# RMSNorm with a sigmoid gate on one core: two row groups of 48 and 16 become 44 and 20

## The chip, the core and the metric

The kernel runs on one NeuronCore of a Trainium2 chip. The metric is device time in microseconds (us), the median of several runs of the whole program. The profile gives one execution: its span runs from the first to the last profiled instruction, and the time of that same execution is a little longer.

Of the engines, four matter here. ACT (ScalarE) and DVE (VectorE) do the arithmetic, POOL (GpSimd) does two small operations for each unit of rows, and SP (SyncE) does no arithmetic: it issues DMA transfers and waits on semaphores. The transfers themselves are run by 16 DMA engines. The tensor engine is not used.

## The reference

```python
def reference(x, gamma, eps):              # x: 16 x 1024 x 512 float32, gamma: 512 ones, eps 1e-5
    rms = np.sqrt(np.mean(x ** 2, axis=-1, keepdims=True) + eps)
    x_norm = x / rms * gamma
    return (x_norm * (1.0 / (1.0 + np.exp(-x_norm)))).astype(np.float32)
```

There are 16384 rows of 512 float32, 2 KB each: 33.55 MB are read and 33.55 MB are written.

## The kernel before

**Tiling.** Each of the 128 partitions holds 128 rows of 2 KB. These rows are cut into *groups* (line 28): 32, 48, 16 and 32 rows. A group of n rows is one block of DRAM, and partition p owns the n rows that follow each other there from p times n on (`dram`, line 100). So n also sets how far apart in DRAM the data of neighbouring partitions lie, the *pitch*: 32 rows are 64 KB, 48 rows 96 KB, 16 rows 32 KB. In SBUF the rows lie in a ring of 96 row slots, `xb` (lines 29 and 108): row 96 takes the slot of row 0. All is done in place.

**Transfers.** `loads` and `stores` (lines 30 to 32) list pieces as (first row, rows); a piece may not cross the edge of a group (the assertion in `dram`). Every piece is one DMA over all 128 partitions; n rows of a partition are contiguous in DRAM and in SBUF. In the text, load 64 is the piece that begins at row 64, store 0 the store that begins at row 0, and so on.

**SP's order** (`order`, lines 33 to 37) is written out by hand. SP issues loads 0, 4 and 8, gamma, then loads 16 to 75. Then it waits until load 64 has landed (line 166), issues store 0 (line 121) and, right behind it, load 80. It waits until store 0 is done, since loads 96 to 125 go into the slots of rows 0 to 31 (line 169), and issues these three. It waits until load 112 has landed and issues the other five stores. Store t waits, besides, until all units that it touches are finished (`ends`, line 56, on the semaphore `s_swish`). At the end SP waits for all stores (line 170).

**Units.** The arithmetic goes by units of 8 rows, 16 units in all. For a unit, ACT squares and sums 6 of its rows (line 215) and DVE the other 2 (line 251; the first unit is split 4 and 4); POOL adds eps and raises to the power -0.5 (lines 183 and 189); DVE multiplies each row by its factor and by gamma (line 260); ACT runs Silu over the whole unit (lines 225 and 245). ACT squares unit k+2 ahead of the Silu of unit k. PE's queue does nothing but wait, for each unit k, for the loads that begin within it, and pass that on to ACT as `s_land`.

The change touches the lists in lines 28 to 37; everything else is worked out from them.

Of the kernel before, what the change touches and what calls it, by code (L numbers as in the profile page):

```python
# [9 lines left out]
def kernel(  # L10
# [14 lines left out]
    of = out.flatten_outer_dims()  # L25
    R, D = xf.shape

    groups = [32, 48, 16, 32]
    ring = 96
    loads = [(0, 4), (4, 4), (8, 8), (16, 8), (24, 8), (32, 16), (48, 16), (64, 11), (75, 5)]  # L30
    loads += [(80, 16), (96, 16), (112, 13), (125, 3)]
    stores = [(0, 32), (32, 32), (64, 16), (80, 16), (96, 24), (120, 8)]
    order = [("load", a) for a in (0, 4, 8)] + [("gamma", 0)]
    order += [("load", a) for a in (16, 24, 32, 48, 64, 75)]
    order += [("landed", 64), ("store", 0), ("load", 80)]
    order += [("stored", 0), ("load", 96), ("load", 112), ("load", 125)]
    order += [("landed", 112)] + [("store", a) for a in (32, 64, 80, 96, 120)]
    early = 2
    cn = 8
    own = 2  # L40
# [285 lines left out]
```

## Time and profile before

| what | us |
|---|---|
| median of 3 runs | 159.67 (159.59 to 159.82) |
| the profiled execution, its own time | 159.75 |
| its span, first to last instruction | 158.4 |
| busy in the span: DVE, ACT, POOL | 107.7, 115.7, 42.9 |

The trace also holds each DMA packet: start, duration and bytes. In this kernel a packet is the rows of one piece for one partition, so a piece has 128 packets, 8 on each of the 16 DMA engines. The next table is put together from these records, by size and order of time; times are from the span's start.

| piece | rows | first packet starts, us | last packet ends, us | packet: median ns | mean ns |
|---|---|---|---|---|---|
| load 0 | 4 | 1.02 | 4.38 | 309 | 367.6 |
| load 4 | 4 | 4.11 | 7.03 | 309 | 310.7 |
| load 24 | 8 | 16.23 | 21.62 | 611 | 611.2 |
| load 32 | 16 | 21.09 | 31.33 | 1215 | 1215.9 |
| load 48 | 16 | 30.77 | 41.04 | 1217 | 1216.7 |
| load 64 | 11 | 40.48 | 47.74 | 840 | 840.6 |
| load 75 | 5 | 47.18 | 50.84 | 389 | 388.7 |
| store 0 | 32 | 50.27 | 70.31 | 2418 | 2448.9 |
| load 80 | 16 | 69.82 | 80.46 | 1213 | 1225.2 |
| load 96 | 16 | 79.53 | 90.14 | 1213 | 1214.4 |
| load 112 | 13 | 89.21 | 98.02 | 987 | 988.8 |
| load 125 | 3 | 97.10 | 99.87 | 234 | 235.1 |
| store 32 | 32 | 99.32 | 119.19 | 2422 | 2430.3 |
| store 64 | 16 | 118.74 | 128.87 | 1218 | 1217.5 |
| store 80 | 16 | 128.45 | 138.55 | 1220 | 1220.9 |
| store 96 | 24 | 138.20 | 153.05 | 1820 | 1820.8 |
| store 120 | 8 | 152.74 | 157.91 | 611 | 613.2 |

The 16 engines don't run in step. The column of first starts follows the engine that is furthest ahead, that of last ends the one that is furthest behind; the first is below the line above's last end because the engines are apart by 0.3 to 0.9 us. All packets together took 2510.5 us, 156.9 us for each of the 16 engines.

### The profile page before, as it was taken

To read this page: it belongs to the slowest core of one execution; us is meant where nothing else is said; L and a number is where in the kernel's file an instruction comes from. 1 tells how busy PE (TensorE), PEld (TensorE's weight loads), DVE (VectorE), ACT (ScalarE), POOL (GpSimd) and SP (SyncE) were. 2 spreads that over 40 slices of the span, in tenths; PEclk is the share of its full clock that TensorE was granted. 3 is DMA by queue.
4 is the path that set the end of the run, shared out by engine and by line. 5 is a ranking of instruction groups with operands and counts; after the bars stand their busy time and mean duration, and the time that the engine had idled before them with its cause. 6 is when DMAs were issued, how large, how long until landed. Compare 5 with 4: busy or idle time off the path is not lost. (4 is left out here: it accounts for less than half of the span.)

```text
span 158.4 us, 844 instructions
## 1 busy us (share of the span) xinstructions
DVE 107.7 (68%) x198; ACT 115.7 (73%) x205; POOL 42.9 (27%) x38
## 2 busy tenths in 40 slices
DVE  0051899798989889898925989989898995000000
ACT  3608389999999999999459999999999385400000
POOL 1031426060524426060601433516061500000000
DMA  7999999999999979799999999996969999999997
GB/s 257 451 416 443 422 488 439 397 406 497 389 395 565 463 331 530 314 381 480 406 406 472 399 430 400 550 513 281 530 298 488 406 397 455 538 397 397 397 397 331
DMA packets 2744, 67.12 MB, mean 424 GB/s; under 512 B 308, under 2 KB 308, under 8 KB 440
## 3 DMA queue, kind: packets, MB, share of 16 engines
q1 hardware_dynamic: 2744, 67.12, 99.1%
HBM read 33.56 MB, written 33.55 MB: 424 GB/s over the span
## 5 line engine op out<-in xcount | busy, mean ns | idle before, releaser
L260 DVE SCALAR_TENSOR_TENSOR xb<-xb,rstd,gamma_sb 128x512 f32 (+1 forms) x128 | 86.1, 745 | 0.0
L215 ACT ACTIVATE junk<-xb 128x512 f32 (+1 forms) x94 | 54.6, 581 | 13.1 <-ACTq L98 11.3
L225 ACT ACTIVATE xb<-xb x14 | 50.5, 3604 | 0.7 <-ACTq L98 0.7
L251 DVE SCALAR_TENSOR_TENSOR junk_v<-xb 128x512 f32 (+1 forms) x34 | 22.1, 689 | 23.0 <-DVEq L98 23.0
L189 POOL TENSOR_TENSOR rstd<-aeps,neg_half 128x8 f32<-128x8 f32 x16 | 31.7, 1984 | 1.3
L183 POOL TENSOR_SCALAR aeps<-ms 128x8 f32<-128x8 f32 x16 | 10.4, 648 | 79.1 <-DVE junk_v L251 79.1
L215 ACT ACTIVATION_READ_ACCUMULATOR junk<-xb 128x1 f32 x94 | 17.7, 188 | 0.0
L245 ACT ACTIVATE xb<-xb 128x4096 f32<-128x4096 f32 x2 | 7.2, 3616 | 5.0 <-DVE xb L260 5.0
L251 DVE DVE_READ_ACCUMULATOR junk_v<-xb 128x1 f32 x34 | 2.8, 82 | 0.0
L227 ACT ACT_TABLE_LOAD x1 | 1.3, 1283 | 1.9 <-PEq L62 1.9
L269 DVE LOAD_MASK_SELECT gamma_sb<-gamma x1 | 0.0, 14 | 2.0 <-DMA gamma<-in_gamma_dram 2.0
L178 POOL MEMSET gamma<- 128x512 f32 x1 | 0.5, 524 | 1.5 <-POOLq L62 1.5
L269 DVE STREAM_SHUFFLE gamma_sb<-gamma 128x512 f32<-128x512 f32 x1 | 0.7, 719 | 0.0
L307 POOL MEMSET const-float32-0.0<- 128x1 f32 x1 | 0.1, 98 | 0.2 <-issue 0.2
L179 POOL MEMSET neg_half<- 128x8 f32 x1 | 0.1, 104 | 0.0
L307 POOL MEMSET const-bfloat16-1.0<- 128x1 bf16 x1 | 0.1, 103 | 0.0
L307 POOL MEMSET const-uint8-127<- 128x1 uint8 x1 | 0.1, 102 | 0.0
L307 POOL MEMSET const-float32-1.0<- 128x1 f32 x1 | 0.1, 99 | 0.0
## 6 DMA issues: line engine op xcount, KB each, us to landing
xb<-in_x_dram SPq DMA_DIRECT2D x4, 4096.0 KB, 29.9
out_dram<-xb SPq DMA_DIRECT2D x2, 4096.0 KB, 29.8
xb<-in_x_dram SPq DMA_DIRECT2D x3, 2048.0 KB, 14.1
out_dram<-xb SPq DMA_DIRECT2D x1, 6144.0 KB, 22.4
xb<-in_x_dram SPq DMA_DIRECT2D x1, 3328.0 KB, 27.0
xb<-in_x_dram SPq DMA_DIRECT2D x1, 2816.0 KB, 43.1
xb<-in_x_dram SPq DMA_DIRECT2D x2, 1024.0 KB, 6.0
out_dram<-xb SPq DMA_DIRECT2D x1, 2048.0 KB, 21.9
```

The source lines that it names most:

```text
L178: nc.gpsimd.memset(gamma4, 0.0).then_inc(s_zero, 1)
L179: nc.gpsimd.memset(neg_half, -0.5).then_inc(s_half, 1)
L183: nc.gpsimd.tensor_scalar(out=aeps[k % 2], in0=ms[min(k, 1)], scalar1=eps_f, scalar2=None, op0=ALU.add,),
L189: nc.gpsimd.tensor_tensor(out=rstd[:, k * cn : (k + 1) * cn], in0=aeps[k % 2], in1=neg_half, op=ALU.pow),
L215: nc.scalar.activation(out=dummies[j], in_=rows[j], func=AF.Square, scale=inv_d**0.5, accum_out=sums[:, j : j + 1],)
L225: nc.scalar.activation(out=rows, in_=rows, func=AF.Silu).then_inc(s_swish, 1)
L227: nc.scalar.preload_act_table_set("silu_and_others")
L245: nc.scalar.activation(out=rows, in_=rows, func=AF.Silu), s_norm, n + 1
L251: ins = nc.vector.scalar_tensor_tensor(out=junk_v[j], in0=rows[j], scalar=inv_d, in1=rows[j], op0=ALU.mult, op1=ALU.mult, accum_out=to[:, ...
L260: ins = nc.vector.scalar_tensor_tensor(out=rows[j], in0=rows[j], scalar=factors[j], in1=gamma_sb, op0=ALU.mult, op1=ALU.mult,)
L269: need(nc.vector.stream_shuffle(gamma_sb, gamma4, [0] * 32), s_gld, 16).then_inc(s_gamma, 1)
L307: nc = _bacc.Bacc("TRN2", target_bir_lowering=False, num_devices=1)
```

## The change

Rows 32 to 79 and 80 to 95, the second and third group, become rows 32 to 75 and 76 to 95. The pitch of the second group goes from 96 KB to 88 KB, that of the third from 32 KB to 40 KB. Load 64 has 12 rows instead of 11, and the load behind it has 4 rows from row 76 on instead of 5 from row 75 on; it is now the beginning of the third group. Load 80 is as long as before, but covers rows 4 to 19 of a group of 20 instead of a whole group. The stores of rows 64 to 95 are 12 and 20 rows instead of 16 and 16. The numbers of loads, stores and waits and their order are the same.

```diff
-    groups = [32, 48, 16, 32]
+    groups = [32, 44, 20, 32]
     ring = 96
-    loads = [(0, 4), (4, 4), (8, 8), (16, 8), (24, 8), (32, 16), (48, 16), (64, 11), (75, 5)]
+    loads = [(0, 4), (4, 4), (8, 8), (16, 8), (24, 8), (32, 16), (48, 16), (64, 12), (76, 4)]
     loads += [(80, 16), (96, 16), (112, 13), (125, 3)]
-    stores = [(0, 32), (32, 32), (64, 16), (80, 16), (96, 24), (120, 8)]
+    stores = [(0, 32), (32, 32), (64, 12), (76, 20), (96, 24), (120, 8)]
     order = [("load", a) for a in (0, 4, 8)] + [("gamma", 0)]
-    order += [("load", a) for a in (16, 24, 32, 48, 64, 75)]
+    order += [("load", a) for a in (16, 24, 32, 48, 64, 76)]
     order += [("landed", 64), ("store", 0), ("load", 80)]
     order += [("stored", 0), ("load", 96), ("load", 112), ("load", 125)]
-    order += [("landed", 112)] + [("store", a) for a in (32, 64, 80, 96, 120)]
+    order += [("landed", 112)] + [("store", a) for a in (32, 64, 76, 96, 120)]
```

## The prediction

> **What bounds the kernel now.** I read first the page's busy times, slices and DMA queue, then SyncE's waits, then the windows around the two places where loads give way to stores.
>
> ```profile
> DVE 107.7 (68%) x198; ACT 115.7 (73%) x205; POOL 42.9 (27%) x38
> DMA  7999999999999979799999999996969999999997
> q1 hardware_dynamic: 2744, 67.12, 99.1%
> ```
>
> No compute engine is busy for more than 73% of the span, while the packets of the one DMA queue took 99.1% of what 16 DMA engines have. A slice (3.96 us) counts a packet where it starts, so the dips of the DMA row at 55 to 67 and 107 to 119 us, among the longest packets (2.4 us), need not be idle time. To tell these apart I counted, from the packet records, how many packets were in flight at each moment. From 2 us to 99 us and from 99.6 us to 157.6 us the mean is 16.0, with no loss. The engines have nothing to do for the first 1.02 us; at 99.0 to 99.6 us they lose 0.12 us of 16 engines' time; and the last packet ends at 157.92. So the span is 1.02 (first issue to first packet) + 156.9 (packets, mean of the engines) + 0.46 (last packet to SyncE's last wait), which is 158.38; the execution's own 159.75 has 1.37 more around the span, and stands 0.08 above the median of 159.67. To change the time one has to change the sum of the packets, or starve the engine that is furthest behind.
>
> ```profile
> SPq L166 <- DMA xb<-in_x_dram: 68.3, 2, 42.1
> SPq L121 <- ACT xb L245: 25.9, 2, 20.9
> SPq L115 <- DMA out_dram<-xb: 21.8, 1, 21.8
> SPq L121 <- ACT xb L225: 10.5, 1, 10.5
> ```
>
> SyncE's own waits: L166 is the wait for a landed load, 42.1 us for load 64 and 26.1 for load 112. These and the wait for store 0 (L115, 21.8) hold SyncE back, but the queue behind it is full meanwhile. The stores' waits for ACT (L121) are for the last three stores, issued at 109.8, 131.1 and 136.4 us; the packet table has their first packets at 128.45, 138.20 and 152.74, so the closest of them is 7.1 us early. ACT's work is hidden there.
>
> ```profile
> 48.37 0.35 SPq L121 DMA_DIRECT2D out_dram<-xb  x1
> 98.48 38.26 SPq L121 DMA_DIRECT2D out_dram<-xb  x5
> xb<-in_x_dram SPq DMA_DIRECT2D x1, 2816.0 KB, 43.1
> xb<-in_x_dram SPq DMA_DIRECT2D x1, 1280.0 KB, 45.7
> ```
>
> The first two lines are from the timeline of SyncE: store 0 is issued at 48.37, store 32 at 98.48. The other two, from the issues, are load 64 (2816 KB), which lands 43.1 us after its issue at 5.13, so at 48.2, and load 75 (1280 KB).
>
> **The change part by part.** *Sizes.* A packet's duration goes linearly with its rows: 8 rows 611 ns, 13 rows 987, so 75.2 ns a row. Load 64 with 12 rows: 987 - 75.2 = 911.8 ns; 8 packets on each engine are 7.29 us, against 8 x 840.6 = 6.72: it ends 0.57 later. The load behind it, 4 rows: load 4's 310.7 x 8 = 2.49 us, against 8 x 388.7 = 3.11. Together 9.78 against 9.83: -0.05 us. Stores: from 8 rows (613.2) to 16 (1217.5) a row is 75.5 ns, so 12 rows are 915 and 20 rows 1519; 8 x 2434 = 19.48 us, against 8 x (1217.5 + 1220.9) = 19.51: -0.03 us. The number of packets stays, and so do their bytes. Sum of the sizes: -0.08 us.
>
> *The first switch to stores.* Its wait changes hands. ACT's Silu of unit 3 runs 44.75 to 48.35 and the landing was at 48.27, so store 0 waited for both alike; now the landing comes at 48.27 + 0.57 = 48.84 and decides. SyncE begins store 0 some 0.1 us later, at 48.94 (before 48.37), and load 80, queued behind it, moves as well from 48.77 to 49.34. How soon could store 0 begin? Where the queue had run dry, at the second switch, its first packet came 99.32 - 98.48 = 0.84 us after the issue: so from 49.78 on. The engine furthest ahead began load 75 at 47.18; now it begins the 4 rows at 47.75 and is through with them at 50.24. A margin of 0.46 us is left of the 1.06 (50.27 against 48.37 + 0.84), and the engine furthest behind has 0.6 more. Price on the path: 0. If the cover is gone: each further us of delay in the landing costs about 0.5 us. Load 80 has the 19 us of store 0 as its cover, then.
>
> *Compute.* Units 8 and 9 wait for loads 64 and 76, both landed by about 51.4; ACT squares unit 8 from 62.62 and unit 9 from 69.80, 11 us later. Unit 10 waits for load 80, whose end doesn't move. Price 0.
>
> *The stores of rows 64 to 95.* Both pieces need the same units as before (through unit 9, and through unit 11), so SyncE issues them at the same times, right behind store 32 and at 109.83. The second comes up 4 x 75.5 x 8 = 2.4 us earlier, at 126.0 instead of 128.45, still 16 us after its issue. The stores behind it keep their places. Price 0.
>
> *The pitch.* No row has 88 or 40 KB. The nearest rows are the same 16-row packets at 96 KB (load 48, 1216.7), at 64 KB (load 96, 1214.4) and at 32 KB (load 80, median 1213, mean 1225.2): the medians are within 0.3%, and the mean of load 80 is raised by its first packets, right behind the last writes of store 0. Store rows say the same: 1217.5 at 96 KB, 1220.9 at 32 KB. The bound against the change is load 80 over load 96, 0.9%, or store 0's mean over its median, 1.3%; the bound for it is that these excesses vanish: (2448.9 - 2418) x 8 = 0.25 us at store 0, 0.10 at load 80, 0.10 at store 32, 0.45 in all. I take 0, since medians at three pitches agree.
>
> [...]
>
> Sum: the execution's own 159.75 - 0.08 = 159.67; less the 0.08 by which it stood above the median, 159.6 us.
>
> **The rivals.** *A, the pitch costs (slower).* At the new pitch the 16 streams of a piece fall into each other's way in DRAM. The place is every packet of rows 32 to 95: 39.1 us of loads (8 x the means of loads 32 to 80) and 39.0 of stores, 78.1 in all. At 0.9% it is 0.7 us, 160.3; at 1.3%, 1.0 us, 160.6. It decides from 0.32 / 78.1 = 0.4%, 5 ns in a 16-row packet. For it: nothing hides it, since no engine is ever idle. Against it: rates at 32, 64 and 96 KB agree. *B, the cover is too short (slower).* If landing and issue take over 1 us longer than here, all engines starve before store 0; 1 us longer idles them by some 0.5 us: 160.2. Against it: at the second switch the cover is shorter still (3 rows, 1.88 us), and the loss there, 0.12 us, falls on the engines ahead, while the one furthest behind went on to 99.87 with no gap. *C, the turn is smoother (faster).* The 0.25 and 0.10 us lost at store 0's end and load 80's start (67 to 71 us) go, because load 80 begins elsewhere in DRAM: 159.3. For it: the excess is real, on nearly all engines. Against it: the turn from writes to reads stays in the program.
>
> **How the numbers follow.** Within 0.2% is 0.32 us, about what a measurement of this kernel can tell, as the three runs are 0.23 apart. The forecast, no change, gets 0.45. A gets 0.29 and B 0.08, together slower 0.37. C gets 0.18. The likeliest case's own range is 159.4 to 159.9. The range goes down to 159.2 (all 0.45 us won back) and up to 160.7 (A at 1.3%), and leaves out some 0.15, most of it above.
>
> **What would show it.** Right: SyncE's store 0 begins at about 48.9, its first packets still at about 50.2; packets of load 64 near 912 ns, of store 76 near 1519; packets in flight stay at 16 through 47 to 71 us; the last packet ends near 157.9. Rival A would show 16-row packets of loads 32 and 48 above 1222 ns; B a hole before store 0's first packets; C a mean of store 0 near 2418. I am wrong if the median leaves 159.35 to 160.0, above all with packets unchanged in length.

## The result, and the profile after

The changed kernel takes 160.26 us (median; 160.09 to 160.41 over 7 executions), the kernel before 159.73 over its 7. The ratio is 1.0033, 95% interval 1.0023 to 1.0043: slower by 0.53 us, where no change was forecast. The profiled execution took 160.11 us, with a span of 158.7; it is 0.36 us longer than that of the kernel before (159.75), and its last packet ends 0.45 us later.

Three parts of the page of the changed kernel: busy times, the DMA row in 40 slices, the DMA queue.

```profile
DVE 107.7 (68%) x198; ACT 115.7 (73%) x205; POOL 42.8 (27%) x38
...
DMA  7999999999999969959999899999969979999997
...
q1 hardware_dynamic: 2744, 67.12, 99.0%
```

Nothing here tells the two kernels apart: the same work, the same 2744 packets, a queue that is as full. The loss has to be looked for in time. SyncE's timeline and two of its waits, changed kernel:

```profile
48.64 0.35 SPq L121 DMA_DIRECT2D out_dram<-xb  x1
49.03 23.23 SPq L115 DMA_DIRECT2D xb<-in_x_dram  x4
98.94 38.24 SPq L121 DMA_DIRECT2D out_dram<-xb  x5
```

```profile
SPq L166 <- DMA xb<-in_x_dram: 69.2, 2, 42.6
...
SPq L115 <- DMA out_dram<-xb: 21.5, 1, 21.5
```

Store 0 is issued 0.27 us later than before (48.64 against 48.37), since the landing of the longer load 64 now comes last. By the second switch, SyncE is 0.46 us late (98.94 against 98.48). In between lies the arrival of load 80, for which ACT waits ahead of unit 10. First ACT's timeline in the kernel before, then in the changed one (start, duration, instruction, idle time ahead of it):

```profile
80.96 0.60 ACT L215 ACTIVATE junk<-xb 128x512 f32 x1 [3.88 <-ACTq L98]
```

```profile
81.41 0.60 ACT L215 ACTIVATE junk<-xb 128x512 f32 x1 [4.65 <-ACTq L98]
```

Load 80 is 0.45 us late there. The DMA queue in the stretch in which store 0 gives way to load 80 (window from 67 to 73 us; length, busy times with instructions, tensor clock, DMA share and GB/s, counted by the packets that start in it), before and after:

```profile
67.00:73.00 6.00, 6.00 (x12) 6.00 (x12) 2.68 (x2) 1.00 1.05 431
```

```profile
67.00:73.00 6.00, 5.84 (x10) 6.00 (x12) 2.68 (x2) 1.00 1.07 415
```

The engines are as busy, and they move less: packets are longer. By the packets in flight, an engine stands idle for only 0.04 us in the mean from 66 to 73 us. The packet records say which packets are longer. As in the table of the kernel before:

| piece | last packet ends, us: before, after | packet mean ns: before, after |
|---|---|---|
| loads 32, 48 | 31.33, 31.07; 41.04, 40.78 | 1215.9, 1215.6; 1216.7, 1216.7 |
| load 64 (11, 12 rows) | 47.74, 48.09 | 840.6, 915.8 |
| load 75 / 76 (5, 4 rows) | 50.84, 50.58 | 388.7, 313.3 |
| store 0 | 70.31, 70.38 | 2448.9, 2467.7 |
| load 80 | 80.46, 80.89 | 1225.2, 1249.0 |
| load 96 | 90.14, 90.58 | 1214.4, 1213.0 |
| load 125 | 99.87, 100.31 | 235.1, 234.0 |
| store 32 | 119.19, 119.63 | 2430.3, 2428.8 |
| stores 64 and 80 / 76 | 138.55, 138.99 | 1217.5 and 1220.9, 915.3 and 1521.8 |
| store 120 | 157.91, 158.36 | 613.2, 612.6 |

For the engine that is furthest behind, all the difference arises between the ends of load 76 and of load 80: it enters 0.26 us earlier and leaves 0.43 us later, and it stays 0.44 us late to the end. (The 0.26 us are there from load 32 on, ahead of all that the change moves.)

Within store 0 and load 80 it is narrower still. All the packets of this kernel take close to 9 ns + 75.26 ns a row when nothing disturbs them (8 rows 611, 16 rows 1213, 32 rows 2417). What exceeds this, as a mean over the 16 engines, for the eight packets of store 0 in turn, is 9, 4, 2, 4, 4, 3, 3 and 224 ns before, and 11, 4, 2, 5, 3, 4, 5 and 368 ns after; for the first packet of load 80 it is 71 and 232 ns. So it is the last packet of store 0, on nearly every engine, and the first of load 80, on about half of them. These two excesses together are called the *turn excess* below: 0.30 us before, 0.60 us after.

The mean engine loses something more at the second switch. SyncE issues store 32 only when load 112 has landed, and the engine furthest behind ends load 112 at 98.46 instead of 98.02. The engines ahead of it run dry meanwhile: by the packets in flight from 97.5 to 102 us, an engine stands idle for 0.33 us in the mean, against 0.12 before. So for the mean engine the loss is 0.30 us at the turn and another 0.21 there; it enters the turn 0.09 us early and ends 0.45 us late.

### The profile page after: what moved, and what is told of

It reads as the page before. It is cut to its first block, busy times and chain, and to the rows that moved or that the text cites. A ratio compares the mean times of both kernels' runs of the same rounds, so it can differ in the third digit from the quotient of the medians.

```text
span 158.7 us, 844 instructions
## 1 busy us (share of the span) xinstructions
DVE 107.7 (68%) x198; ACT 115.7 (73%) x205; POOL 42.8 (27%) x38
## 2 busy tenths in 40 slices
DMA packets 2744, 67.12 MB, mean 423 GB/s; under 512 B 308, under 2 KB 308, under 8 KB 440
## 3 DMA queue, kind: packets, MB, share of 16 engines
q1 hardware_dynamic: 2744, 67.12, 99.0%
```

## The experiments

The names in capitals in the expectations are rival causes, and each expectation says what every one of them would show. LEAD was put forward only after the first four runs. The *lead* is the time from SyncE's issue of store 0 to the first packet of store 0. It is 50.27 - 48.37 = 1.89 us before (unrounded) and 50.27 - 48.64 = 1.63 after. Ratios are to the kernel before, timed on the same chip beside each kernel; the packet values are from one profiled execution each. The code cuts show the lines that matter; where pieces change, `order` names their new first rows.

| kernel | lead, us | turn excess, us | ratio (95%) |
|---|---|---|---|
| before | 1.89 | 0.30 | |
| changed | 1.63 | 0.60 | 1.0033 (1.0023 to 1.0043) |
| e1_pieces | 1.21 | 0.65 | 1.0024 (1.0014 to 1.0033) |
| e2_load80_back | 1.33 | 0.54 | 1.0023 (1.0014 to 1.0032) |
| e3_layout | 1.98 | 0.19 | 0.9993 (0.9982 to 1.0003) |
| e4_step | 0.84 | 0.90 | 1.0134 (1.0118 to 1.0150) |
| e5_store0_late | 1.83 | 0.38 | 1.0009 (0.9998 to 1.0020) |
| e6_load80_late | 2.15 | 0.13 | 1.0015 (1.0005 to 1.0026) |
| e7_load80_later | 2.05 | 0.15 | 0.9994 (0.9985 to 1.0004) |
| e8_more_ahead | 5.07 | 0.005 | 1.0058 (1.0043 to 1.0072) |
| f1_after_no_landing | 2.17 | 0.19 | 1.0001 (0.9991 to 1.0011) |
| f2_before_delay | 1.22 | 0.66 | 1.0023 (1.0014 to 1.0033) |
| f3_six_ahead | 2.61 | 0.05 | 0.9992 (0.9983 to 1.0001) |
| f4_eight_delay | 2.12 | 0.28 | 1.0009 (1.0000 to 1.0017) |

Runs e1 to e4 share one chip, e5 to e8 another and f1 to f4 a third. Within each of these sets a longer lead goes with a smaller turn excess, without exception. The ratios of the changed kernel, e1, e2 and f2 cannot be told apart: their intervals overlap. The idle time at the second switch is less regular: 0.26 us in e1, about 0.14 in e2 and f2, 0.03 in f1.

**The parts of the change apart.** In e1_pieces the kernel before gets the two loads alone.

```diff
-    loads = [..., (64, 11), (75, 5)]
+    loads = [..., (64, 12), (76, 4)]
```

> Only the two loads are 12 and 4 rows; groups and stores are those of before. Theory LAYOUT (load 80 reads from a less favourable place in DRAM while the last writes of store 0 drain): as before, ratio 0.999 to 1.001, mean packet of load 80 near 1225 ns, of store 0 near 2449. Rival TIMING (store 0 and load 80 are issued 0.3 us later, with a shorter cover): as the changed kernel, ratio near 1.003, mean of load 80 near 1249 ns, of store 0 near 2468. Rival STEP (the 16 engines reach the turn more in step): ratio near 1.003 only if the last packets of store 0 start within 0.4 us of each other instead of 0.57.

It is slower, and its turn excess is near that of the changed kernel.

```profile
49.03 0.35 SPq L121 DMA_DIRECT2D out_dram<-xb  x1
```

Store 0 is issued at 49.03 here, later than in the changed kernel's profile, with the same pieces: the two executions had their loads some 0.4 us apart by then.

e2_load80_back leaves the place of load 80 in DRAM as it was, and the late issue in:

```diff
-    groups = [32, 44, 20, 32]
+    groups = [32, 44, 4, 16, 32]
-    stores = [(0, 32), (32, 32), (64, 12), (76, 20), (96, 24), (120, 8)]
+    stores = [(0, 32), (32, 32), (64, 12), (76, 4), (80, 16), (96, 24), (120, 8)]
```

> Groups 32, 44, 4, 16 and 32: load 80 has its old place and pitch (32 KB) in DRAM, the 4 rows from 76 on are a group of their own, and the stores of rows 64 to 95 are 12, 4 and 16. LAYOUT of load 80: as before, ratio 0.999 to 1.001, load 80 near 1225 ns. TIMING: ratio near 1.003, load 80 near 1249 ns, since store 0 is issued as late as in the changed kernel. STEP: by the spread of the starts of store 0's last packets.

It is as slow as e1_pieces. e3_layout is the reverse: all of the new groups and stores, and the early landing back.

```diff
-    loads = [..., (64, 12), (76, 4)]
+    loads = [..., (64, 11), (75, 1), (76, 4)]
```

> Groups and stores of the changed kernel, but load 64 has 11 rows again and the 5 rows behind it are loads of 1 and 4 rows, so store 0 is issued at about 48.4. LAYOUT: as the changed kernel, ratio 1.003, load 80 near 1249 ns. TIMING: as before, 0.999 to 1.001 (up to 0.05 us more for the packets of one more load, 8 x 9 ns).

Its ratio is 0.9993. So the 88 and 40 KB pitches and the stores of 12 and 20 rows cost nothing that can be measured, with one more load besides, and layout falls as a cause. What is left is when store 0 and load 80 are issued, or how far the engines are in step.

e4_step lets the queue run dry before store 0:

```diff
-    order += [("landed", 64), ("store", 0), ("load", 80)]
+    order += [("landed", 75), ("store", 0), ("load", 80)]
```

> The kernel of before, but SyncE waits for load 75 instead of load 64 before it issues store 0. All engines run dry and begin store 0 together. The hole costs about 0.55 us (landing) + 0.1 + 0.84 (issue to first packet) = 1.5 us for the engine furthest behind. STEP: store 0's last packets start within 0.15 us of each other and the turn costs more than in the changed kernel: store 0 above 2468 ns, load 80 above 1249, time 161.6 or more. LAYOUT and TIMING: turn as before (2449 and 1225 ns), time near 161.1.

The time was 161.96. Of the excess over the kernel before, the hole itself has most (a mean of 1.6 us for the engines around 51 us); the turn, 20 us later, has the dearest excess of all, 0.90 us, as STEP expected and TIMING, as it was worded, did not. But STEP doesn't order the others: the last packets of store 0 start within 0.36 us of each other in the changed kernel and within 0.67 in e1_pieces, with a turn excess of 0.60 and 0.65; and within 0.57 in the kernel before, with 0.30. The lead orders them better.

**Store 0's lead or load 80's.** e5_store0_late puts eight more waits that are already met ahead of store 0, e6_load80_late puts them between store 0 and load 80, and e7_load80_later puts a real wait there.

```diff
# e5_store0_late
+    order += [("landed", 64)] * 9 + [("store", 0), ("load", 80)]
# e6_load80_late
+    order += [("landed", 64), ("store", 0)] + [("landed", 64)] * 8 + [("load", 80)]
# e7_load80_later
+    order += [("landed", 64), ("store", 0), ("landed", 75), ("load", 80)]
```

> The kernel of before with its own pieces (11 and 5 rows); SyncE goes through eight more waits that are already met before it issues store 0, so store 0 and load 80 are issued some 0.4 to 0.8 us later. Theory LEAD (what counts is how long before its turn the 16 queues hold store 0 and load 80; the turn from store 0 to load 80, 67 to 72 us, is dearer for a shorter lead): ratio 1.002 to 1.004, turn excess (store 0's eighth packets and load 80's first ones) above 0.5 us against 0.35. Rival PIECES (a 12-row piece with 4 rows behind it costs by itself): ratio 0.999 to 1.001.

> The kernel of before; the eight met waits stand between store 0 and load 80, so only load 80 is issued 0.4 to 0.8 us later. LEAD of store 0: as before, 0.999 to 1.001, turn excess near 0.35 us. LEAD of load 80: 1.002 to 1.004, turn excess above 0.5 us.

> The kernel of before; SyncE waits for load 75 between store 0 and load 80, so load 80 is issued at about 51.5 instead of 48.8, after store 0's first packets have begun. LEAD of store 0: turn excess near 0.35 us, ratio near 1. LEAD of load 80: turn excess 0.9 us or more (the kernel in which both were issued at 51.2 to 51.6 showed 1.0), ratio 1.004 or more.

SyncE's timeline of e7:

```profile
47.98 0.35 SPq L121 DMA_DIRECT2D out_dram<-xb  x1
51.07 20.90 SPq L115 DMA_DIRECT2D xb<-in_x_dram  x4
```

e7 answers the question: load 80 was issued at 51.07, after store 0 had begun, and the turn excess is 0.15 us, the ratio 0.9994. Load 80's own lead doesn't matter, as far as it was moved here (2.3 us later than in the kernel before). e5 missed its aim: the waits took 60 ns a pair, the landing had come early (47.85), and store 0 went out only 0.23 us later than in e6 (48.16 against 47.93). Its turn excess is larger than e6's (0.38 against 0.13), which is in order, but the time is not clear of no change. Its profile also has a mean of 0.47 us of idle engines at the second switch, where those of e6 and e7 have none. e6 is a miss of another kind: its profiled execution (159.46) shows a small turn excess, while its ratio says slightly slower. Its executions lie in two groups, seven from 159.43 to 159.54 and five from 159.89 to 160.14, and the profile is of the first group; what the longer ones have is not known.

**More rows ahead.** e8_more_ahead lengthens the lead by a longer cover in the changed kernel:

```diff
-    loads = [..., (64, 12), (76, 4)]
-    loads += [(80, 16), ...]
+    loads = [..., (64, 12), (76, 8)]
+    loads += [(84, 12), ...]
```

> Groups, stores and load 64 of the changed kernel, but the load behind it takes 8 rows instead of 4, and the load behind store 0 is 12 rows from row 84 on. Store 0 is issued as in the changed kernel (48.6 to 49.0), its first packets come 2.5 us later, at 52.7. LEAD: 3.6 us or more of lead, turn excess at most 0.35 us, ratio at or below 1.000. PIECES, or an effect of the issue's time alone: 1.002 to 1.004, turn excess 0.6 us or more.

Half right. The turn excess vanished (0.005 us), and yet the kernel is the slowest but for e4_step. SyncE's timeline:

```profile
48.56 0.35 SPq L121 DMA_DIRECT2D out_dram<-xb  x1
48.95 26.56 SPq L115 DMA_DIRECT2D xb<-in_x_dram  x4
```

Store 0's first packet was expected at 52.7 and came at 53.64. The records show why: packets of 8 rows that begin up to 50.45 take 611 to 619 ns, all but one; those from 50.60 on, 2.04 us after the issue of store 0, take 622 to 1349 ns, all but the very last (608), 1.2 us for each engine in all. So the store that was issued long before its turn slowed the loads that were still ahead of it. A place in the queue alone doesn't do that: in the changed kernel loads 64 and 76 were issued 35 and 42 us ahead of their turn, and load 48 ahead of them took its 1216.7 ns.

**Lead, pieces and DRAM place.** The next four separate these. f1_after_no_landing is the whole change without SyncE's wait for load 64, so that ACT alone releases store 0; f2_before_delay is the kernel before with a longer string of met waits; f3_six_ahead lies between the changed kernel and e8; f4_eight_delay is e8 with store 0 held back.

```diff
# f1_after_no_landing, from the changed kernel
-    order += [("landed", 64), ("store", 0), ("load", 80)]
+    order += [("store", 0), ("load", 80)]
# f2_before_delay, from the kernel before
+    order += [("landed", 64)] * 25 + [("store", 0), ("load", 80)]
# f3_six_ahead, from the changed kernel
+    loads = [..., (64, 12), (76, 6)]
+    loads += [(82, 14), ...]
# f4_eight_delay, from e8_more_ahead
+    order += [("landed", 64)] * 61 + [("store", 0), ("load", 84)]
```

> The changed kernel without SyncE's wait for load 64 ahead of store 0, which then waits for ACT alone and is issued at about 48.0 to 48.4 instead of 48.6 to 49.0. LEAD (time from the issue of store 0 to its first packet; the profiles so far give a turn excess of 0.13 us at a lead of 2.15, 0.30 at 1.89, 0.60 at 1.63, 0.65 at 1.21, 0.90 at 0.84): lead 1.9 to 2.2, turn excess 0.1 to 0.3 us, ratio 0.999 to 1.001. PIECES (12 and 4 rows cost by themselves): ratio 1.002 to 1.004 as in the changed kernel.

> The kernel of before, pieces of 11 and 5 rows, with 24 more waits that are already met ahead of store 0 (they took 60 ns a pair in an earlier run), so that store 0 is issued about 0.6 us later. LEAD: about 1.2 to 1.4, turn excess 0.5 to 0.7 us, ratio 1.002 to 1.004. PIECES: as before, ratio 0.999 to 1.001, turn excess up to 0.3 us.

> The changed kernel with 6 rows behind load 64 and 14 behind store 0 (instead of 4 and 16): the lead is 2.5 to 2.9 us. LEAD: turn excess at most 0.13 us. The kernel with 8 rows there had a turn excess of 0.005 us, but its loads ahead of store 0 ran 1.2 us slow from 2.0 us after the issue of store 0 on. If that comes with a lead above 2.0 us, its price here is the lead above 2.0, 0.5 to 0.9 us times some 0.35: 0.2 to 0.35 us, ratio 0.999 to 1.002. If it belongs to the place of these rows in DRAM, their last packets are as slow as there whenever store 0 is issued.

> The kernel with 8 rows behind load 64 (ratio 1.0058, lead 5.1), with 60 more waits that are already met ahead of store 0, so that it is issued near 50.6 and the lead is again about 2 us. LEAD: the loads ahead of store 0 run at full speed (no packet of 8 rows above 650 ns), turn excess 0.1 to 0.4 us, ratio 0.999 to 1.002. DRAM place: the packets from 50.6 us on are slow as before, ratio 1.004 to 1.007.

The issue of store 0 in SyncE's timelines of f1, f2 and f4, in this order:

```profile
48.11 0.35 SPq L121 DMA_DIRECT2D out_dram<-xb  x1
```

```profile
48.97 0.35 SPq L121 DMA_DIRECT2D out_dram<-xb  x1
```

```profile
50.59 0.35 SPq L121 DMA_DIRECT2D out_dram<-xb  x1
```

f1 and f2 are the decisive pair. The full change with store 0 issued at 48.11 costs nothing (1.0001); the kernel before, unchanged but for an issue at 48.97, costs 0.23%, with a turn excess near that of the changed kernel. The pieces don't matter by themselves, the issue does. f4 differs from e8 only in the 60 waits, which put off store 0 and load 84 behind it: no packet of its loads ahead is slow, the turn costs 0.28 us again, and the ratio falls from 1.0058 to 1.0009. So a long string of waits costs nothing by itself, and e8's loss isn't the place of these rows in DRAM. f3, at a lead of 2.61, pays a little on both sides: 0.18 us by slow loads at 49 to 52 us and 0.05 at the turn. Its 0.9992 is the lowest of the table with e3 and e7, and not clear of no change; it is the version that the experiments pointed to, and it does not beat the kernel before by more than can be told.

## Why the prediction was wrong, point by point

- **What bounds the kernel**: right. The DMA engines are full, the loss began in the packets, and it reached the end undiminished: 0.43 us at the end of load 80, 0.45 at the last packet.
- **Sizes**: right for the single packets. 12 rows of load 64 were put at 911.8 ns and took 915.8, store 76 was put at 1519 and took 1521.8. Their sum was put at -0.08 us and came to -0.01: rows 64 to 79 took 9.83 us of each engine in both kernels, the two stores 19.50 instead of 19.51.
- **The first switch to stores**: here it failed. The step said that the landing would decide, that store 0 would be issued near 48.9 (48.64 in the profile, 49.03 in e1_pieces, with the same pieces), and that a margin of cover would be left: the order of events and the margin were true, and no engine starved between 47 and 53 us. From this it set "Price on the path: 0", on the assumption that a store issued later, but still in time, costs nothing. What the runs showed in its place: with 0.27 us less of lead, the turn from store 0 to load 80, some 20 us later, costs 0.30 us more (mean of the engines), and the second switch 0.21 more behind it. f2_before_delay, the kernel before with nothing but a later issue, loses 0.23% and has a turn excess of 0.66 us. The step's words on load 80, that it has store 0 as its cover, took for granted that a covered switch is free; this switch is not.
- **Compute, the stores of rows 64 to 95**: right in that neither decides; e3_layout has the stores and no cost.
- **The pitch** and rival A: the zero taken was right. Loads 32 and 48, at the new pitch, are unchanged at 1215.6 and 1216.7 ns, and e3_layout bears it out in time. Load 80's median is 1213 ns at both pitches; its mean rose by the packets at the turn. (Of the 0.45 us that could at most be won, the 0.10 at store 32 are 0.07 by its own median, 2422.) The Trainium skill (DMA: Bandwidth & Descriptors, Latency and other measured facts) lists slow copies at row pitches that are large powers of two, 103 GB/s at 4 and 8 MiB against 214 with 4 KiB of padding. No run here has such a pitch; 40 KB instead of 32 KB won nothing.
- **The number**: 160.26 left the 159.35 to 160.0 beyond which the prediction called itself wrong. It lies within the wider range and beside rival A's 160.3, but that is coincidence. A would have spread the loss over every packet of rows 32 to 95; it fell on one turn and on the switch behind it.
- **Rival B**: it looked at the right switch, and its mechanism was wrong: the cover was not too short, and there was no hole before store 0.
- **Rival C**: it named the turn as the place where 0.35 us could be won. The turn does move, but with the lead and not with load 80's place in DRAM, and here it went the other way, as e2_load80_back shows: the old place, the same cost.

What stays open is how the lead acts. If the DMA engines started on store 0's reading side some time after its issue, ahead of its turn, this would fit both findings: too early, it takes from the loads that are still running (e8), and too late, it isn't ahead when load 80's reads have to begin. The Trainium skill (DMA: Bandwidth & Descriptors, Two DMAs through the same engine are not ordered) says that reading and writing are separate queues within an engine, which allows this. No run here looks inside an engine, so it is argued, not shown. The time of that start is no constant: nearly all slow loads begin 2.0 us after the issue and later in e8, most from 1.3 us on in f3, and f1, with a lead of 2.17 us, has none.

Why e6_load80_late, with a small turn excess at a lead near 2 us, was no faster is open as well. Even its profile, of a short execution, has slow loads ahead of store 0, 0.12 us for each engine after the issue at 47.93; but 19 packets were over 20 ns slow before it, so the store can't be the only reason.

## What to carry to other kernels

Even while a DMA queue doesn't run dry, the moment at which a transfer is issued can have a price, though its cover holds: here a store issued 1.2 to 1.6 us ahead of its turn instead of 1.9 cost 0.2 to 0.3% at the next turn, and one issued 5 us ahead cost 0.6%. A split of loads ahead of a wait is therefore a timing knob and not only a cover; change it together with the wait that it feeds, and look at the first and last packets of each turn, not at the mean of a queue. When a late stage loses, look back to what was issued late one stage earlier.

## What the runs showed of the hardware that was not expected

- The turn from a store to a load costs time on nearly all 16 DMA engines, most of it in the last packet of the store and the first of the load: 0.005 us for each engine at a lead of 5.07, 0.05 at 2.61, 0.13 to 0.30 at 1.89 to 2.17, 0.38 at 1.83, 0.54 to 0.66 at 1.21 to 1.63, 0.90 at 0.84. The issue that sets it lies some 20 us earlier, with seven almost undisturbed packets between (at most 11 ns each, but for 58 in the first of e4).
- In e8 a store waiting in the queue slowed the loads ahead of it, nearly all of them from 2.04 us after its issue on: packets of 8 rows took up to 1349 ns for 611. With the store held back (f4) none took more than 619.
- Apart from that and from the first microseconds, a packet's duration is 9 ns + 75.26 ns for each 2 KB row, from 3 to 32 rows, reads or writes, at pitches of 32, 40, 64, 88 and 96 KB, to within some 1%.
